# Weight block sums and residual additions moved from VectorE to accumulating DMAs, in a hybrid decoder layer on one Trainium2 core

## The chip, the core and the metric

The kernel runs on one core of one Trainium2 chip. A core has TensorE (PE: matmuls, with weight loads, PEld, running beside them), VectorE (DVE), ScalarE (ACT), GpSimd (POOL) and SyncE (SP), each with its own in-order queue of instructions; waits between them are semaphores. DMAs are issued from SP (all loads of weights) and from POOL, and run on 16 DMA engines.

The metric is the device time in microseconds. The kernel before takes 1687.98 us (median of three runs, 1686.88 to 1688.58).

## The reference

One decoder layer on 256 tokens of width 2048, all in float32:

```
x = layer_norm(ALPHA*x + 0.5 * swiglu_ffn(x, ffn1 weights))       # D_FF = 5632
u = x @ w_in + b_in ;  attention on 16 heads | conv module on 1024 channels
x = layer_norm(ALPHA*x + concat(attention, conv) @ w_out + b_out)
x = layer_norm(ALPHA*x + 0.5 * swiglu_ffn(x, ffn2 weights))
swiglu_ffn(x, g, u, d) = (silu(x @ g) * (x @ u)) @ d
```

Most of the arithmetic is in the two FFNs: per FFN three products with 2048 x 5632 weights.

## The kernel before

**Three matmuls per product.** Every float32 operand is split into a rounded part `hi` and a rest `lo = x - hi`. A product is hi*hi + hi*lo + lo*hi, three matmuls in the function `mm3` (L624 to L626). The split of a weight tile of 128 x 1024 costs one ScalarE cast (`upper`, L153: hi) and one VectorE subtraction (`lower`, L157: lo). Both halves go into rings of eight tiles; TensorE reads them from there.

**Seven products in place of eight.** In most of both FFNs the matrices are taken in 2 x 2 blocks. A step of kind "C" is the plain one: two weight tiles, eight block products. A step of kind "S" is a Strassen-like one: seven products, for which sums of the weights' blocks and of the activations' blocks are needed. One call of `by_sums` runs eight such steps with two of kind "S" (SCCSCCCC, once CCSCSCCC): 62 products in eight PSUM banks. A call computes either two groups of the up product (`pair`) or half of a down product's columns (`down_by_sums`). There are 28 calls, so 56 sets of weight tiles for "S" steps.

**A set.** `load_set` loads two weight tiles: one into `raw` (blocks a0 | a1), one into `rawx` (b0 | b1). Out of these VectorE makes the operands in four subtractions (`sub`, L171): t0 = b0 - a0, t1 = b1 - t0 (tiles `sum`), b0 = b1 - b0 in place in `rawx`, a1 = a1 - t1 in place in `raw`. The operands are taken in the order U0 = a0 | a1, U1 = t0 | t1, U2 = the changed rawx, U3 = the changed a1; each is split into hi and lo like any weight tile. Four buffers of kind `raw` are shared by all loads; a buffer is loaded anew when its last split is done (`ended`, `load`).

**What sets the order.** The class `Steps` writes out the order by hand. `jobs` is the list of splits still to be done, `pending` holds a `lo` until the next tile's `hi` has been queued, and `pace` takes jobs while a running estimate of VectorE's backlog is below a limit. `soon` holds short pieces of work (additions, the splits of activations) that `pace` slips in between; `at(n, work)` puts work n steps ahead. `can` lets a tile be split up to seven tiles ahead of the one in use.

**Evictions.** When a call's second "S" step has ended, `shared` combines the four banks that only "S" steps fill: in `pair` with VectorE additions at L1002 into tiles `part`, in `down_by_sums` with L881 into `part`, followed by four VectorE additions of these parts to the residual `xt` (`plus`, L885). The other four banks are added at the end of the call (L1002, L881). The next call's products reuse the banks.

**Activations.** At the end of a `pair` ScalarE applies silu to the parts (L1018), VectorE multiplies gate and up side (L949) and transposes 32 x 32 blocks (`turn`, L963), and POOL takes the result through DRAM: four DMAs `far<-hr` (L968) and one `hf<-far` (L970). Six steps later VectorE splits `hf` into `hh`, `hl` (L926, L977).

Of the kernel before, what the change touches and what calls it, by code (L numbers as in the profile page):

```python
# [74 lines left out]
class Steps:  # L75
# [6 lines left out]
    def __init__(self, nc, pool, sources, head, pooled, xT, x_raw, xcat):  # L82
# [3 lines left out]
        self.jobs, self.ready, self.pending, self.sets = [], {}, [], 0  # L86
        self.later, self.background, self.backlog = [], None, 0.0
# [24 lines left out]

    def load(self):
        while self.open < RAW_BUFS and self.loaded < len(self.sources):
            n = self.loaded
            if isinstance(self.sources[n], tuple):
                if self.sets == 2:
                    return
                self.load_set(n)
                continue  # L120
# [13 lines left out]
            self.jobs.append(("free", None, None))  # L134

    def load_set(self, n):
# [6 lines left out]
        for i, work in enumerate((self.zeroth, self.first, self.second, self.third)):  # L143
            self.jobs.append((n + i, raws, work))

# [24 lines left out]
    def sub(self, out, a, b):  # L170
        self.nc.vector.tensor_tensor(out=out, in0=a, in1=b, op=ALU.subtract)  # L171
        self.vector(0.6)

    def zeroth(self, n, raws):
        zero = self.upper(n, raws[0])
        self.flush()
        raws.append(zero)

    def first(self, n, raws):
        a, b = ([r[:, :512], r[:, 512:]] for r in raws[:2])  # L180
        t = [self.act.tile([P, 512], F32, tag="bc", name=f"sum{n}", bufs=BC) for _ in range(2)]
        raws.append(t)
        self.sub(t[0], b[0], a[0])
        self.sub(t[1], b[1], t[0])
        self.pending = [raws[2], self.upper(n, t)]

    def second(self, n, raws):
        b = [raws[1][:, :512], raws[1][:, 512:]]
        self.sub(b[0], b[1], b[0])
        self.pending.append(self.upper(n, raws[1]))  # L190
        self.flush(1)

    def third(self, n, raws):
        a1 = raws[0][:, 512:]
        self.sub(a1, a1, raws[3][1])
        three = self.upper(n, a1)
        self.flush(1)
# [7 lines left out]
        self.pending.append(ended)  # L205
# [124 lines left out]
def hybrid_layer(  # L330
# [534 lines left out]
    def down_by_sums(hh, hl, kinds, factor):  # L865
# [11 lines left out]
        for c in range(0, NC_, 2):  # L877
            ys = {(i, j): xt[:, 1 - i, (c + j) * 512 : (c + j + 1) * 512] for i in range(2) for j in range(2)}

            def add(out, ps, other):  # L880
                nc.vector.scalar_tensor_tensor(out=out, in0=ps, scalar=factor, in1=other, op0=ALU.mult, op1=ALU.add)  # L881
                st.vector(0.62, 0.3)

            def plus(y, t):
                nc.vector.tensor_tensor(out=y, in0=y, in1=t, op=ALU.add)  # L885
                st.vector(0.6)

            def shared(bank, ys=ys):
# [4 lines left out]
                add(tmp[3], bank[5], tmp[1])  # L893
                add(ys[1, 1], bank[5], ys[1, 1])
# [603 lines left out]
```

## Time and profile before

| | |
|---|---|
| median of three runs | 1687.98 us |
| the profiled execution's own time | 1688.99 us |
| its span, first to last instruction | 1687.2 us |
| granted TensorE clock, mean | 0.998 |
| DVE busy | 1386.7 us (82%), 2035 instructions |
| ACT busy | 912.9 us (54%) |
| POOL busy | 268.1 us (16%), nearly all between 680 and 980 us |
| DMA, mean rate | 213 GB/s |

A matmul's record is longer than the distance to the next matmul's start, because matmuls are pipelined and their ends are modelled; a busy share of TensorE therefore hides short stalls, and counting matmuls in a stretch shows them better. An entry such as "idle before 9.3 <-ACT hi" says how long the engine stood before the instructions of a group, and who ended most of it.

### The profile page before, as it was taken

Reading aid. Unit: us, or ns where it says so; the run is one execution under the profiler, and the core shown is the slowest. Engines: PE = TensorE matmul, PEld = TensorE weight load, DVE = VectorE, ACT = ScalarE, POOL = GpSimd, SP = SyncE. Lnnn points to the kernel's source line nnn. Section 1 sums busy time; section 2 is a strip of 40 time slices with the busy share of each in tenths; the row PEclk is TensorE's granted clock in tenths of the full one; section 3 lists DMA queues with packets and bytes.
Section 4 is the critical chain, followed back from the end, with each engine's and each line's share of the span. In section 5 each row is a group of like instructions: output and inputs, shape, how many; then the busy total and the mean of one; then the engine's idle time right before and its main releaser. Section 6 shows DMA issues by size and latency. Waiting matters only on the chain.

```text
span 1687.2 us, 21755 instructions
## 1 busy us (share of the span) xinstructions
PE 1669.7 (99%) x7689; PEld 1383.6 (82%) x7689; DVE 1386.7 (82%) x2035; ACT 912.9 (54%) x1252; POOL 268.1 (16%) x226
## 2 busy tenths in 40 slices
PE   9999999999999999999999999999999999999997
PEld 7887788888888888888888888877888888888886
DVE  7888898789888886758887778998888888988866
ACT  6556555555555554576665465555545555545541
POOL 0100000000000000178996200000000000000000
PEclk9999999999999999999999999999999999999999
DMA  8767666567666667556654555776656665666682
GB/s 295 241 211 271 219 209 218 191 223 244 214 215 211 212 213 246 171 182 194 200 181 157 198 193 196 246 236 210 219 200 215 221 237 202 222 200 224 209 279 99
DMA packets 103694, 359.47 MB, mean 213 GB/s; under 512 B 12960, under 2 KB 13088, under 8 KB 103328
## 3 DMA queue, kind: packets, MB, share of 16 engines
q1 hardware_dynamic: 96048, 334.74, 58.6%
q0 software_dynamic: 7392, 23.08, 4.5%
q8 instruction: 60, 0.98, 0.2%
q14 instruction: 50, 0.41, 0.1%
q10 hardware_dynamic: 144, 0.26, 0.0%
HBM read 344.40 MB, written 13.63 MB: 212 GB/s over the span
## 4 chain that ended last, share of the span: by engine, by line
PE 67%; DVE 19%; DMA 6%; issue 5%; ACT 3%; DVEq 0%; POOL 0%; ACTq 0%; SPq 0%; POOLq 0%
PE sum L624 13%; PE sum L625 13%; PE sum L626 13%; DVE lo L157 9%; PE acc L624 4%; PE acc L626 4%; PE acc L625 4%; DMA raw<-in_wu 3%; ACT hi L153 2%; DVE part L1002 2%; DVE sum L171 2%; PE in_c L1149 2%; PE in_a L1149 2%; PE in_q L1149 1%; DMA raw<-in_wd 1%
## 5 line engine op out<-in xcount | busy, mean ns | idle before, releaser
L157 DVE TENSOR_TENSOR lo<-raw,hi 128x1024 fp32r<-128x1024 f32 x452 | 506.6, 1153 | 121.5 <-ACT hi L153 121.0
L153 ACT CAST hi<-raw 128x1024 fp32r<-128x1024 f32 x452 | 432.9, 996 | 298.9 <-DMA raw<-in_wu 108.1
L624 PE MATMUL sum<-hi,xcat 128*128 128x512 f32 x1080 | 420.4, 389 | 1.6 <-DVE part L1002 1.6
L625 PE MATMUL sum<-lo,xcat 128*128 128x512 f32 x1080 | 420.3, 389 | 0.6 <-DVE lo L157 0.6
L626 PE MATMUL sum<-hi,xcat 128*128 128x512 f32 x1080 | 420.2, 389 | 0.0
L624 PEld LDWEIGHTS sum<-hi,xcat 128*128 128x128 f32 x1080 | 202.7, 188 | 44.7 <-DVE part L1002 2.5
L625 PEld LDWEIGHTS sum<-lo,xcat 128*128 128x128 f32 x1080 | 202.7, 188 | 42.9 <-DVE lo L157 1.0
L626 PEld LDWEIGHTS sum<-hi,xcat 128*128 128x128 f32 x1080 | 202.7, 188 | 42.2
L968 POOL DMA_DIRECT2D far<-hr x88 | 48.8, 556 | 1167.3 <-DVE hr L963 1120.9
L236 ACT CAST hi<-raw 128x1024 fp32r<-128x1024 f32 (+1 forms) x164 | 166.6, 1030 | 119.9 <-PE acc L626 71.8
L624 PE MATMUL sum<-hi,hh 128*128 128x512 f32 x496 | 194.0, 391 | 1.9 <-DVE part L1002 1.3
L239 POOL TENSOR_TENSOR lo<-raw,hi 128x1024 fp32r<-128x1024 f32 x73 | 175.6, 2423 | 117.5 <-ACT hi L236 110.6
L626 PE MATMUL sum<-hi,hl 128*128 128x512 f32 x496 | 193.1, 389 | 0.0
L625 PE MATMUL sum<-lo,hh 128*128 128x512 f32 x496 | 193.0, 389 | 0.0
L153 ACT CAST hi<-sum 128x512 fp32r<-128x512 f32 x112 | 69.5, 622 | 139.1 <-DVE sum L171 128.9
L239 DVE TENSOR_TENSOR lo<-raw,hi 128x1024 fp32r<-128x1024 f32 (+1 forms) x91 | 106.9, 1203 | 37.9 <-ACT hi L236 37.1
L1002 DVE TENSOR_TENSOR part<-sum,part 128x512 f32<-128x512 f32 x160 | 105.1, 685 | 12.7 <-PE sum L626 8.1
L624 PEld LDWEIGHTS sum<-hi,hh 128*128 128x128 f32 x496 | 93.1, 188 | 25.1 <-DVE part L1002 3.5
L626 PEld LDWEIGHTS sum<-hi,hl 128*128 128x128 f32 x496 | 93.1, 188 | 19.4
L625 PEld LDWEIGHTS sum<-lo,hh 128*128 128x128 f32 x496 | 93.1, 188 | 18.8
L1212 DVE SCALAR_TENSOR_TENSOR conv<-hc,cw_sb,conv 128x256 f32<-128x256 f32 x231 | 96.6, 482 | 1.1
L153 ACT CAST hi<-rawx 128x1024 fp32r<-128x1024 f32 x56 | 59.0, 1053 | 48.9 <-DVE rawx L171 39.3
(198 smaller groups left out, 2319.2 us busy)
## 6 DMA issues: line engine op xcount, KB each, us to landing
raw<-in_wu SPq DMA_DIRECT2D x308, 512.0 KB, 4.8
raw<-in_wd SPq DMA_DIRECT2D x160, 512.0 KB, 4.7
raw<-in_win SPq DMA_DIRECT2D x52, 512.0 KB, 4.1
rawx<-in_wu SPq DMA_DIRECT2D x40, 512.0 KB, 6.3
raw<-in_wout SPq DMA_DIRECT2D x32, 512.0 KB, 3.7
far<-hr POOLq DMA_DIRECT2D x88, 128.0 KB, 2.7
hf<-far POOLq DMA_DIRECT2D x22, 512.0 KB, 3.6
rawx<-in_wd SPq DMA_DIRECT2D x16, 512.0 KB, 6.4
```

The costliest lines, as they stand in the source:

```text
L153: self.nc.scalar.copy(hi, x_)
L157: self.nc.vector.tensor_tensor(out=lo, in0=x_, in1=hi.bitcast(F32), op=ALU.subtract)
L171: self.nc.vector.tensor_tensor(out=out, in0=a, in1=b, op=ALU.subtract)
L236: nc.scalar.copy(hi, raw)
L239: eng.tensor_tensor(out=lo, in0=raw, in1=hi.bitcast(F32), op=ALU.subtract)
L624: nc.tensor.matmul(ps, s_hi, m_hi, start=start, stop=False)
L625: nc.tensor.matmul(ps, s_hi, m_lo, start=False, stop=False)
L626: nc.tensor.matmul(ps, s_lo, m_hi, start=False, stop=stop)
L968: nc.gpsimd.dma_start(far[:, :, t].rearrange("f r n -> r f n"), hr[32 * t : 32 * t + 32])
L1002: nc.vector.tensor_tensor(out=out, in0=ps, in1=other, op=ALU.add)
L1149: nc.tensor.matmul(ps, w[0][:, n], x1[:, k], start=k == 0, stop=False)
L1212: nc.vector.scalar_tensor_tensor(out=out, in0=x_, scalar=w, in1=acc, op0=ALU.mult, op1=ALU.add)
```

## The change

The block sums get other signs, so that all of them are additions on the weights' side: t0 = a0 + b0 and t1 = t0 + b1 stay on VectorE (now `plus`, L183), b0 += b1 (in `rawx`) and a1 += t1 (in `raw`) become DMAs from SBUF to SBUF that add to their destination, issued on POOL's queue (L192 and L200 of the changed kernel). The activations' sums and the combination of the banks have their signs changed to fit, with as many instructions as before. In `down_by_sums` the four additions to the residual become four such DMAs (L912); the addition of bank 5 to the residual becomes one more part, so the number of L881 additions is the same.

The order changes with it. The two sums of a set are placed two weight tiles earlier. U3's split is held back until the next load has been put on the list, so it stands one weight tile later. Every `lo` now stays pending until the next tile's `hi` is queued. The DMAs through DRAM are queued one and three steps after the transpose in place of at once, and the split of `hf` after seven steps in place of six. Counted over the program, VectorE has 1893 instructions in place of 2037, POOL 375 in place of 231, of which 56 are b0 += b1, 56 a1 += t1 and 32 additions to the residual. TensorE's instructions are the same, in the same order.

```
@@ last_third, load
+    def last_third(self):
+        if self.held is not None:
+            self.jobs.append(self.held)
+            self.held = None
...
             if isinstance(self.sources[n], tuple):
                 if self.sets == 2:
                     return
+                self.last_third()
                 self.load_set(n)
                 continue
...
             self.get(raw, n, 0, 1024)
             self.jobs.append(("free", None, None))
+            self.last_third()
@@ load_set
-        for i, work in enumerate((self.zeroth, self.first, self.second, self.third)):
+        early = len(self.jobs) > 3 and self.jobs[-1][0] == "free"
+        at = len(self.jobs) - 2 if early else len(self.jobs)
+        self.jobs.insert(at, (n - early, raws, self.sums))
+        for i, work in enumerate((self.zeroth, self.first, self.second)):
             self.jobs.append((n + i, raws, work))
+        self.held = (n + 3, raws, self.third)
@@ the set's work
-    def sub(self, out, a, b):
-        self.nc.vector.tensor_tensor(out=out, in0=a, in1=b, op=ALU.subtract)
+    def plus(self, out, a, b):
+        self.nc.vector.tensor_tensor(out=out, in0=a, in1=b, op=ALU.add)
         self.vector(0.6)
+
+    def sums(self, n, raws):
+        a, b = ([r[:, :512], r[:, 512:]] for r in raws[:2])
+        t = [self.act.tile([P, 512], F32, tag="bc", name=f"sum{n}", bufs=BC) for _ in range(2)]
+        raws.append(t)
+        self.plus(t[0], a[0], b[0])
+        self.plus(t[1], t[0], b[1])
+        self.nc.gpsimd.dma_start(b[0], b[1], accum_op=ALU.add)
 
     def zeroth(self, n, raws):
         zero = self.upper(n, raws[0])
         self.flush()
-        raws.append(zero)
+
+        def ended():
+            zero()
+            self.nc.gpsimd.dma_start(raws[0][:, 512:], raws[2][1], accum_op=ALU.add)
+
+        self.pending = [ended]
 
     def first(self, n, raws):
-        a, b = ([r[:, :512], r[:, 512:]] for r in raws[:2])
-        t = [self.act.tile([P, 512], F32, tag="bc", name=f"sum{n}", bufs=BC) for _ in range(2)]
-        raws.append(t)
-        self.sub(t[0], b[0], a[0])
-        self.sub(t[1], b[1], t[0])
-        self.pending = [raws[2], self.upper(n, t)]
+        one = self.upper(n, raws[2])
+        self.flush()
+        self.pending = [one]
 
     def second(self, n, raws):
-        b = [raws[1][:, :512], raws[1][:, 512:]]
-        self.sub(b[0], b[1], b[0])
-        self.pending.append(self.upper(n, raws[1]))
-        self.flush(1)
+        two = self.upper(n, raws[1])
+        self.flush()
+        self.pending = [two]
 
     def third(self, n, raws):
-        a1 = raws[0][:, 512:]
-        self.sub(a1, a1, raws[3][1])
-        three = self.upper(n, a1)
-        self.flush(1)
+        three = self.upper(n, raws[0][:, 512:])
+        self.flush()
@@ down_by_sums
                 tmp = [act.tile([P, 512], F32, tag="z", name="part", bufs=ZB) for k in range(4)]
                 nc.scalar.mul(tmp[0], bank[1], factor)
                 add(tmp[1], bank[6], tmp[0])
-                add(tmp[3], bank[5], tmp[1])
-                add(ys[1, 1], bank[5], ys[1, 1])
+                add(tmp[3], bank[5], tmp[1], ALU.subtract)
                 add(tmp[2], bank[7], tmp[1])
-                for n, (at, k) in enumerate((((0, 0), 0), ((0, 1), 3), ((1, 0), 2), ((1, 1), 2))):
-                    st.soon.append(lambda y=ys[at], t=tmp[k]: plus(y, t))
+                add(tmp[1], bank[5], tmp[2], ALU.subtract)
+                for at, k in ((0, 0), 0), ((0, 1), 3), ((1, 0), 2), ((1, 1), 1):
+                    nc.gpsimd.dma_start(ys[at], tmp[k], accum_op=ALU.add)
@@ turn
-                    for t in range(4):
-                        nc.gpsimd.dma_start(far[:, :, t].rearrange("f r n -> r f n"), hr[32 * t : 32 * t + 32])
+                    def leave():
+                        for t in range(4):
+                            nc.gpsimd.dma_start(far[:, :, t].rearrange("f r n -> r f n"), hr[32 * t : 32 * t + 32])
+
                     hf = pool.tile([P, 8 * P], F32, tag="ht", name="hf")
-                    nc.gpsimd.dma_start(hf, far.rearrange("f r t n -> (f r) (t n)"))
+                    st.at(1, leave, True)
+                    st.at(3, lambda: nc.gpsimd.dma_start(hf, far.rearrange("f r t n -> (f r) (t n)")), True)
...
-                    st.at(6, lambda: st.soon.extend([lambda t=t: split(hf, t) for t in range(2)]))
+                    st.at(7, lambda: st.soon.extend([lambda t=t: split(hf, t) for t in range(2)]))
```

The first place is VectorE's queue in the first FFN, where the second `pair` ends: the first set of the third `pair` is split ahead, and the last row is the evictions at the second one's end, for which the third one's products wait. In the names, `lo<-raw` is a tile's split, `sum` is t0 and t1, and the brackets name the semaphores waited for: DMAHW a load's landing, DMASW the landing of a DMA of POOL's queue, Activation, PE and DVE these engines. Before:

```order
L171 TENSOR_TENSOR sum_1161<-rawx_1097,raw_1096 128x512 [waits DMAHW2_49,DMAHW1_49]
L171 TENSOR_TENSOR sum_1162<-rawx_1097,sum_1161 128x512 [waits DVE_49]
L157 TENSOR_TENSOR lo_1150<-raw_1096,hi_1149 128x1024 [waits Activation_49]
L171 TENSOR_TENSOR rawx_1097<-rawx_1097 128x512
L157 TENSOR_TENSOR lo_1166<-sum_1161,hi_1165 128x512 [waits Activation_49]
L157 TENSOR_TENSOR lo_1166<-sum_1162,hi_1165 128x512 [waits Activation_49]
L171 TENSOR_TENSOR raw_1096<-raw_1096,sum_1162 128x512 [waits DVE_49]
L157 TENSOR_TENSOR lo_1181<-rawx_1097,hi_1180 128x1024 [waits Activation_49]
L157 TENSOR_TENSOR lo_1197<-raw_1096,hi_1196 128x512 [waits Activation_49]
L157 TENSOR_TENSOR lo_1216<-raw_1132,hi_1215 128x1024 [waits DMAHW4_49,Activation_49]
L157 TENSOR_TENSOR lo_1236<-raw_1141,hi_1235 128x1024 [waits DMAHW5_49,Activation_49]
L1002 TENSOR_TENSOR part<-sum,part 128x512 [waits PE_49] x3
```

The same place in the changed kernel:

```order
L183 TENSOR_TENSOR sum_1140<-raw_1082,rawx_1083 128x512 [waits DMAHW2_49,DMAHW1_49]
L183 TENSOR_TENSOR sum_1141<-sum_1140,rawx_1083 128x512 [waits DVE_49]
L169 TENSOR_TENSOR lo_1138<-raw_1040,hi_1137 128x1024 [waits DMAHW7_49,Activation_49]
L169 TENSOR_TENSOR lo_1152<-raw_1058,hi_1151 128x1024 [waits DMAHW0_49,Activation_49]
L169 TENSOR_TENSOR lo_1164<-raw_1082,hi_1163 128x1024 [waits Activation_49]
L169 TENSOR_TENSOR lo_1173<-sum_1140,hi_1172 128x512 [waits Activation_49]
L169 TENSOR_TENSOR lo_1173<-sum_1141,hi_1172 128x512 [waits Activation_49]
L169 TENSOR_TENSOR lo_1185<-rawx_1083,hi_1184 128x1024 [waits DMASW2_49,Activation_49]
L169 TENSOR_TENSOR lo_1210<-raw_1087,hi_1209 128x1024 [waits DMAHW3_49,Activation_49]
L169 TENSOR_TENSOR lo_1213<-raw_1082,hi_1212 128x512 [waits DMASW3_49,Activation_49]
L169 TENSOR_TENSOR lo_1236<-raw_1155,hi_1235 128x1024 [waits DMAHW5_49,Activation_49]
L1020 TENSOR_TENSOR part<-sum,part 128x512 [waits PE_49] x3
```

The two in-place sums are gone, the two others stand two tiles earlier, ahead of `lo_1138` and `lo_1152`, and U2 (`lo_1185`) and U3 (`lo_1213`) now wait for DMAs of POOL's queue, U3 with one more tile ahead of it.

The second place is POOL's queue at a call's end in the first FFN. Before, it holds nothing but the way through DRAM:

```order
L968 DMA far<-hr 32x4x256 [waits DVE_49]
L968 DMA far<-hr 32x4x256 x3
L970 DMA hf<-far 128x1024 [waits DMASW6_49,DMASW7_49,DMASW5_49,DMASW0_49]
```

In the changed kernel, from the second set of the second `pair`, which is split while the first one's result passes, to the first set of the third:

```order
L192 DMA rawx_856<-rawx_856 128x512 [waits DMAHW0_49,DMASW6_49,DVE_49]
L984 DMA far<-hr 32x4x256 [waits DVE_49]
L984 DMA far<-hr 32x4x256 x2
L984 DMA far<-hr 32x4x256 [waits DMASW7_49]
L200 DMA raw_855<-sum_919 128x512 [waits DMASW2_49,DMAHW7_49,DMASW0_49,DVE_49]
L988 DMA hf<-far 128x1024 [waits DMASW6_49,DMASW5_49,DMASW7_49,DMASW4_49,DMASW1_49]
L192 DMA rawx_1083<-rawx_1083 128x512 [waits DMAHW2_49,DVE_49]
L200 DMA raw_1082<-sum_1141 128x512 [waits DMAHW1_49,DMASW3_49,DMAHW5_49,DMASW0_49,DVE_49]
```

The addition a1 += t1 (`raw_855<-sum_919`) stands behind the four `far<-hr` issues, and `hf<-far` behind it.

More of the change, by code (lines that the diff above doesn't have):

```diff
@@ L111, in raw @@
         return self.pool.tile([P, 1024], F32, tag="raw", name=f"raw{n}", bufs=RAW_BUFS)
+    def last_third(self):
+        if self.held is not None:
+            self.jobs.append(self.held)
+            self.held = None
     def load(self):
@@ L203, in ended @@
             self.load()
-        self.pending.append(ended)
+        self.pending = [ended]
     def split(self):
@@ L878, in down_by_sums, with add @@
             ys = {(i, j): xt[:, 1 - i, (c + j) * 512 : (c + j + 1) * 512] for i in range(2) for j in range(2)}
-            def add(out, ps, other):
-                nc.vector.scalar_tensor_tensor(out=out, in0=ps, scalar=factor, in1=other, op0=ALU.mult, op1=ALU.add)
+            def add(out, ps, other, op=ALU.add):
+                nc.vector.scalar_tensor_tensor(out=out, in0=ps, scalar=factor, in1=other, op0=ALU.mult, op1=op)
                 st.vector(0.62, 0.3)
-            def plus(y, t):
-                nc.vector.tensor_tensor(out=y, in0=y, in1=t, op=ALU.add)
-                st.vector(0.6)
             def shared(bank, ys=ys):
@@ L922, in block_sums @@
                 for o, y, z, op in (
-                    (out[:, 0], x_[0], x_[2], ALU.add), (out[:, 2], x_[1], x_[0], ALU.subtract),
-                    (out[:, 1], out[:, 0], x_[1], ALU.subtract), (out[:, 3], x_[3], out[:, 1], ALU.subtract),
+                    (out[:, 0], x_[0], x_[2], ALU.subtract), (out[:, 2], x_[1], x_[0], ALU.subtract),
+                    (out[:, 1], out[:, 0], x_[1], ALU.subtract), (out[:, 3], x_[3], out[:, 1], ALU.add),
                 ):
@@ L993, in split, with add @@
                         parted(at + 3, sums)
-                    st.at(6, lambda: st.soon.extend([lambda t=t: split(hf, t) for t in range(2)]))
+                    st.at(7, lambda: st.soon.extend([lambda t=t: split(hf, t) for t in range(2)]))
                 def pair(g, ups):
                     tmp, places = [], {(0, 0): 0, (0, 1): 2, (1, 0): 1, (1, 1): 3}
-                    def add(out, ps, other):
-                        nc.vector.tensor_tensor(out=out, in0=ps, in1=other, op=ALU.add)
+                    def add(out, ps, other, op=ALU.add):
+                        nc.vector.tensor_tensor(out=out, in0=ps, in1=other, op=op)
                         st.vector(0.62, 0.3)
@@ L1009, in shared @@
                         add(tmp[1], bank[6], tmp[0])
-                        add(tmp[2], bank[5], tmp[1])
+                        add(tmp[2], bank[5], tmp[1], ALU.subtract)
                         add(tmp[1], bank[7], tmp[1])
-                        add(tmp[3], bank[5], tmp[1])
+                        add(tmp[3], bank[5], tmp[1], ALU.subtract)
                     def out(at, ps):
```

## The prediction

> **What bounds the kernel now.** First the page's busy times.
>
> ```profile
> PE 1669.7 (99%) x7689; PEld 1383.6 (82%) x7689; DVE 1386.7 (82%) x2035; ACT 912.9 (54%) x1252; POOL 268.1 (16%) x226
> ```
>
> TensorE's 99% is no measure of its pace, since a record (0.39 us) is longer than the distance between two starts. That distance stands in the timeline of a stretch without stalls:
>
> ```profile
> 299.68 0.39 PE L626 MATMUL sum<-hi,xcat 128*128 128x512 f32 x1
> ...
> 300.36 0.39 PE L626 MATMUL sum<-hi,xcat 128*128 128x512 f32 x1
> ```
>
> Three matmuls, one product, in 0.68 us: 0.227 us each. The change leaves TensorE's work alone, so it can win only TensorE's stalls. The table of stretches shows where they are (after PE and (x), the number of matmuls that started or ran there; then PEld, DVE, ACT, POOL, clock, DMA share, GB/s):
>
> ```profile
> 42.20:84.40 42.20, 42.20 (x188) 34.95 (x187) 35.40 (x47) 23.17 (x31) 4.86 (x8) 1.00 0.73 241
> 126.50:168.70 42.20, 41.35 (x181) 33.56 (x180) 36.53 (x47) 26.29 (x31) 2.78 (x5) 1.00 0.75 271
> 168.70:210.90 42.20, 41.60 (x183) 33.73 (x182) 35.48 (x47) 21.59 (x29) 2.77 (x5) 1.00 0.63 219
> 210.90:253.10 42.20, 42.07 (x186) 34.36 (x185) 38.06 (x47) 21.60 (x25) 0.00 (x0) 1.00 0.60 209
> 1054.50:1096.70 42.20, 41.62 (x184) 34.10 (x183) 38.63 (x54) 23.00 (x31) 2.77 (x5) 1.00 0.72 246
> 1096.70:1138.90 42.20, 41.03 (x178) 32.95 (x177) 38.77 (x51) 25.02 (x34) 2.77 (x5) 1.00 0.71 236
> 1138.90:1181.00 42.10, 41.14 (x180) 33.40 (x179) 37.72 (x50) 21.96 (x29) 2.77 (x5) 1.00 0.63 210
> 1181.00:1223.20 42.20, 42.05 (x185) 34.25 (x185) 37.64 (x47) 22.58 (x26) 0.00 (x0) 1.00 0.64 219
> 1645.00:1687.20 42.20, 30.70 (x146) 25.59 (x144) 28.15 (x53) 6.96 (x8) 3.10 (x4) 0.90 0.29 99
> ```
>
> A full stretch holds 187 or 188. The seven short ones lack 6, 4, 1, 3, 9, 7 and 2 against 187: 32 matmuls, 32 x 0.227 = **7.3 us**. That is about all this change can win: the last row's idle time is the final normalisation, which isn't touched, and the other stretches of the FFNs are full. In the short ones VectorE is busy 35.5 to 38.8 us of 42.2, as the rows show, and what TensorE waits for is VectorE's evictions:
>
> ```profile
> 136.05 0.39 PE L626 MATMUL sum<-hi,xs 128*128 128x512 f32 x1
> 137.16 0.50 PE L624 MATMUL sum<-hi,xcat 128*128 128x512 f32 x1 [0.72 <-DVE part L1002]
> ```
>
> VectorE before that moment is hardly ever idle; this is a whole set, from its first block sum to the evictions:
>
> ```profile
> 126.48 0.68 DVE L171 TENSOR_TENSOR sum<-rawx,raw 128x512 f32<-128x512 f32 x1
> ...
> 128.94 0.68 DVE L171 TENSOR_TENSOR rawx<-rawx 128x512 f32<-128x512 f32 x1
> 129.55 1.28 DVE L157 TENSOR_TENSOR lo<-sum,hi 128x512 fp32r<-128x512 f32 x2
> 130.75 0.68 DVE L171 TENSOR_TENSOR raw<-raw,sum 128x512 f32<-128x512 f32 x1
> 131.35 1.22 DVE L157 TENSOR_TENSOR lo<-rawx,hi 128x1024 fp32r<-128x1024 f32 x1
> 133.20 0.69 DVE L157 TENSOR_TENSOR lo<-raw,hi 128x512 fp32r<-128x512 f32 x1 [0.63 <-ACT hi L153]
> 134.15 2.36 DVE L157 TENSOR_TENSOR lo<-raw,hi 128x1024 fp32r<-128x1024 f32 x2 [0.26 <-ACT hi L153]
> 136.43 2.48 DVE L1002 TENSOR_TENSOR part<-sum,part 128x512 f32<-128x512 f32 x4
> 140.33 1.23 DVE L157 TENSOR_TENSOR lo<-raw,hi 128x1024 fp32r<-128x1024 f32 x1 [1.43 <-ACT hi L153]
> ```
>
> The evictions stand behind the splits in VectorE's queue and come 7 us after the first split. So VectorE, late by up to a few microseconds here, is the bound behind TensorE in seven stretches, and nowhere else.
>
> **What is removed.** Two subtractions a set. From start to start one costs 0.6 us (128.94 to 129.55, 130.75 to 131.35), so 1.2 us a set, and 0.6 x 4 = 2.4 us in each down call for the additions to the residual. The groups by shape give their number, and the waits that go with them:
>
> ```profile
> L171 DVE TENSOR_TENSOR rawx<-rawx 128x512 f32<-128x512 f32 x56 | 38.3, 684 | 0.0
> L885 DVE TENSOR_TENSOR xt<-xt,part 128x512 f32<-128x512 f32 x32 | 19.9, 682 | 0.0
> L157 DVE TENSOR_TENSOR lo<-raw,hi 128x512 fp32r<-128x512 f32 x56 | 38.3, 685 | 9.3 <-ACT hi L153 9.3
> L157 DVE TENSOR_TENSOR lo<-rawx,hi 128x1024 fp32r<-128x1024 f32 x56 | 68.3, 1219 | 13.8 <-ACT hi L153 13.7
> L171 DVE TENSOR_TENSOR sum<-rawx,raw 128x512 f32<-128x512 f32 x56 | 37.8, 675 | 11.7 <-DMA rawx<-in_wd 7.1 <-DMA rawx<-in_wu 4.5
> L153 ACT CAST hi<-raw 128x512 fp32r<-128x512 f32 x56 | 34.8, 622 | 63.4 <-DVE raw L171 63.4
> ```
>
> VectorE stands (9.3 + 13.8) / 56 = 0.4 us a set because a tile that it changed itself must first go through ScalarE. These waits go too: **1.6 us a set saved**, two sets a call.
>
> **What is added.** The time of an adding DMA is nowhere in the trace. Nearest are POOL's own DMAs, from issue to landing:
>
> ```profile
> far<-hr POOLq DMA_DIRECT2D x88, 128.0 KB, 2.7
> hf<-far POOLq DMA_DIRECT2D x22, 512.0 KB, 3.6
> ```
>
> The view of the tile `hf` adds its spread:
>
> ```profile
> DMA to landing us min/median/max: 3.4/3.6/5.0
> ```
>
> An adding DMA of 256 KB reads 512 KB, source and destination, so I take 3.6 us, with 2.7 and 5.0 as ends. The addition to U3's half may start once U0's lo is done; until U3's turn VectorE has the two lo of U1 (129.55 to 130.75, 1.2), U2's and the next tile's (1.13 each): 3.5 us of cover. The chain is 3.6 + 0.62 for the half tile's cast: 4.2. VectorE stands 0.8 us, and 0.4 more because the next tile's cast (1.0) only starts behind it on ScalarE while U3's lo takes 0.6: **1.2 us a set**, from 0.2 (landing 2.7) to 2.6 (5.0). Behind that wait in VectorE's queue are the next lo and then the evictions for which TensorE waits. b0 += b1 has more cover (t1, two tiles, U0, U1: over 5 us) and costs nothing up to there.
>
> In a sentence by itself: the Trainium skill, "DMA: Bandwidth & Descriptors", section "Anatomy of one DMA — SWDGE (gpsimd) path", fits such a DMA by 2.0 us + bytes/436 GB/s, which makes an estimate of 2.6 us for 256 KB and would cut the wait to 0.2 us and clear all 7.3 us of stalls; here the fit gives 3.2 and 2.3 where the trace has 3.6 and 2.7, and it does not speak of adding.
>
> **What is moved.** The sums stand two tiles earlier and need the set's loads 2 x 1.13 = 2.3 us sooner. The list of waits (in total, times, longest) shows how many have no such margin today:
>
> ```profile
> DVE sum L171 <- DMA rawx<-in_wd: 7.1, 6, 1.4
> DVE sum L171 <- DMA rawx<-in_wu: 4.5, 7, 1.2
> ```
>
> These 13 of 56 sets pay all of it, 13 x 2.3 / 56 = 0.5 us a set, the others between nothing and 2.3, which no row tells: I take **0.6 us a set** (0.5 to 2.3), near the low end, since 43 sets don't wait at all. In an up call the second set's sums (1.3 us) come to stand right behind the evictions, where VectorE waits 1.43 us for a cast anyway (row 140.33): **1.3 us saved**. On POOL the same set's a1 += t1 stands behind four issues:
>
> ```profile
> L968 POOL DMA_DIRECT2D far<-hr x88 | 48.8, 556 | 1167.3 <-DVE hr L963 1120.9
> ```
>
> Four are 2.2 us, one lo (1.13) of which runs meanwhile: **1.1 us** per up call. `far` and `hf` leave later, and the split of `hf` is a step later; its activations are used only in the down call's last steps, many products on, so I cost that at nothing. U3's raw buffer is free one tile later: nothing while three others are filled, a load's wait if not.
>
> **The sum.** Up call: saved 3.2 + 1.3, new waits 2.4 + 1.2 + 1.1: -0.2, no gain, if every new wait delays VectorE in full. Down call: 3.2 + 2.4 - 2.4 - 1.2 = 2.0 gained. But the short stretches still hold 3.4 to 6.7 us of idle VectorE, so a new wait partly takes the place of one that comes anyway. Charged at half, an up call gains 2.1 us and a down call 3.8. That is more than any short stretch lacks per call (9 matmuls, 2.0 us), so all 7.3 us go. Charged in full, only the stalls behind a down call go, which are the short ones:
>
> ```profile
> PEld sum L624 <- DVE xt L881: 2.1, 5, 0.6
> ```
>
> In the table these are the stretches from 210.90 and 1181.00: 3 matmuls, 0.7 us. I take the middle of 7.3 and 0.7, **4.0 us**: 1688.99 - 4.0 = 1685.0 for a profiled execution; this one lay 1.0 over the median of the runs, so **1684.0 us**.
>
> **Rivals.** *A wash.* Every new wait counts in full, and VectorE is as late at the evictions as now. For it: both engines are in order, and U3's wait stands right ahead of the evictions. Against it: VectorE has half as many instructions for the sums. Gain -2 to 3 us: 1687.0 us.
>
> *Slower: the adding DMA lands late.* At 5.0 us (`hf`'s slowest) U3's wait is 2.6 us. Charged in full an up call loses 3.0 us (4.5 saved, 2 x 2.6 + 2.3 waited) and a down call 0.8; the seven short stretches hold about four up and three down calls: 4 x 3.0 + 3 x 0.8 = 14 us, 1702. At three quarters an up call loses 1.1 us and a down call nothing: 4 us, 1692. I put it at 1697. It decides where the charged waits reach the 4.5 us saved: a landing of 3.5 us in full, of 5.7 us at half. For it: the loads keep the engines two thirds busy (the 0.60 to 0.75 above) and reading the destination may be slower than I assume. The queues' row prices the traffic:
>
> ```profile
> q0 software_dynamic: 7392, 23.08, 4.5%
> ```
>
> (packets, MB, share of the 16 engines.) 144 DMAs of 0.262 MB are 37.7 MB, 7.4% of the engines, 15% with the second read, which takes the busiest short stretch from 0.75 to 0.90, so the engines don't become the bound.
>
> **How the numbers follow.** Within 0.2%, 3.4 us, a measurement of this kernel can't tell a change from none: 1684.6 to 1691.4. The forecast case (half or more of the stalls gone, 1680.5 to 1684.6) gets 0.41, the wash 0.32, slower 0.27. So faster 0.41, same 0.32, slower 0.27. Range: low end all 7.3 us and a little run-to-run, 1679.5; high end into the slower case, 1699. The likeliest case's own range is 1680.5 to 1684.6.
>
> **What would show it.** Right: the seven stretches at 187 matmuls, 144 fewer VectorE instructions (some 95 us less busy: 112 x 0.68 + 32 x 0.68), additions landing in 3 to 4 us, waits of U3's cast on them under 1 us. Wrong: landings of 5 us or more; ScalarE's casts waiting for POOL's DMAs by over 100 us in all; sums waiting for `rawx` far beyond 11.7 us; new short stretches where now there are 188.

## The result and the profile after

The changed kernel takes 1784.89 us (median of four runs, 1782.20 to 1788.64), the kernel before beside it 1688.28 us (four runs, 1686.88 to 1690.10): a ratio of 1.0573, 95% interval 1.0551 to 1.0595. It is **slower by 96.6 us**. The prediction said 1684.0 us, and 1699 at the high end; it was wrong in sign.

The page of the changed kernel: busy times, the queue of GpSimd's DMAs, the first line of the chain that ended last, and GpSimd's issues with their size and the median from issue to landing.

```profile
PE 1703.9 (96%) x7689; PEld 1393.6 (78%) x7689; DVE 1303.6 (73%) x1891; ACT 903.4 (51%) x1252; POOL 395.7 (22%) x370
q0 software_dynamic: 28128, 60.83, 17.0%
PE 32%; DMA 29%; DVE 16%; issue 13%; ACT 5%; POOL 3%; SPq 1%; ACTq 0%; DVEq 0%; POOLq 0%
rawx<-rawx POOLq DMA_DIRECT2D x56, 256.0 KB, 3.6
raw<-sum POOLq DMA_DIRECT2D x56, 256.0 KB, 4.5
xt<-part POOLq DMA_DIRECT2D x32, 256.0 KB, 7.4
```

The edit does what it says: VectorE has 144 instructions fewer and is busy 83 us less (1386.7 before). But the chain now runs through DMAs for 29% of the span; before, it was TensorE for 67% and DMAs for 6%:

```profile
PE 67%; DVE 19%; DMA 6%; issue 5%; ACT 3%; DVEq 0%; POOL 0%; ACTq 0%; SPq 0%; POOLq 0%
```

What the freed VectorE gave is not seen, and new waits are (engine, line and what it waited for; total, times, longest):

```profile
DVE lo L169 <- ACT hi L165: 266.5, 163, 7.7
ACT hi L165 <- DMA rawx<-rawx: 187.9, 53, 10.6
ACT hi L165 <- DMA raw<-sum: 183.2, 44, 7.5
DVE sum L183 <- DMA rawx<-in_wu: 55.3, 30, 5.0
DVE sum L183 <- DMA rawx<-in_wd: 26.5, 16, 3.0
PEld sum L643 <- DVE part L1020: 38.0, 25, 4.3
```

Three things are in it: ScalarE's casts wait 187.9 us for b0 += b1 and 183.2 us for a1 += t1, and the two sums left on VectorE wait 81.8 us for the set's loads, where it was 11.7 before. In the last line TensorE's weight loads wait for evictions, which come later for it. The table of stretches (same columns as in the prediction; a full one of 44.6 us holds 196 to 200 matmuls):

```profile
89.20:133.80 44.60, 39.69 (x159) 31.59 (x160) 34.14 (x43) 18.16 (x25) 5.50 (x9) 0.92 0.76 224
223.00:267.60 44.60, 39.30 (x163) 31.48 (x163) 28.19 (x33) 18.03 (x22) 5.76 (x7) 0.92 0.79 224
579.80:624.40 44.60, 44.60 (x199) 36.93 (x198) 34.28 (x41) 21.61 (x28) 5.77 (x8) 1.00 0.78 232
1248.80:1293.40 44.60, 38.95 (x162) 31.20 (x161) 28.89 (x34) 20.21 (x23) 5.63 (x8) 0.92 0.80 228
```

Of the seven stretches inside the FFNs with the fewest matmuls six lie behind a down call's residual additions; the first row here, the lowest of them, does not. In all seven even the granted clock is below 1.00, which it was nowhere inside the FFNs before. The timeline of a place behind the residual, GpSimd first, then VectorE, ScalarE and TensorE:

```profile
220.60 0.86 POOL L912 DMA_DIRECT2D xt<-part  x1 [9.77 <-ACT part L906]
222.70 1.74 POOL L912 DMA_DIRECT2D xt<-part  x2 [1.23 <-DVE part L900]
230.00 0.88 POOL L912 DMA_DIRECT2D xt<-part  x1 [5.56 <-issue]
230.95 0.87 POOL L192 DMA_DIRECT2D rawx<-rawx  x1
...
227.08 0.69 DVE L183 TENSOR_TENSOR sum<-sum,rawx 128x512 f32<-128x512 f32 x1
239.49 1.23 DVE L169 TENSOR_TENSOR lo<-rawx,hi 128x1024 fp32r<-128x1024 f32 x1 [7.10 <-ACT hi L165]
...
238.41 1.04 ACT L165 CAST hi<-rawx 128x1024 fp32r<-128x1024 f32 x1 [9.98 <-DMA rawx<-rawx]
...
244.24 0.80 PE L643 MATMUL sum<-hi,hh 128*128 128x512 f32 x1 [2.74 <-DVE xt L900]
```

The set's second sum ends at 227.8. b0 += b1 could go then, but GpSimd is still at the residual: it stands 5.56 us between the third and the fourth of those DMAs, with no semaphore to wait for ("issue"). So b0 += b1 is issued at 230.95 and needs 7.3 us to land behind the four transfers; U2's cast is at 238.41, VectorE has stood 7.10 us, and the evictions (`xt`, L900) come so late that TensorE stands too.

### The profile page after: what moved, and what is told of

It is laid out like the page before. It is cut to its first block, busy times and chain, and to the rows that moved or that the text cites. A ratio compares the mean times of both kernels' runs of the same rounds, so it can differ in the third digit from the quotient of the medians.

```text
span 1783.4 us, 22067 instructions
## 1 busy us (share of the span) xinstructions
PE 1703.9 (96%) x7689; PEld 1393.6 (78%) x7689; DVE 1303.6 (73%) x1891; ACT 903.4 (51%) x1252; POOL 395.7 (22%) x370
## 3 DMA queue, kind: packets, MB, share of 16 engines
q0 software_dynamic: 28128, 60.83, 17.0%
## 4 chain that ended last, share of the span: by engine, by line
PE 32%; DMA 29%; DVE 16%; issue 13%; ACT 5%; POOL 3%; SPq 1%; ACTq 0%; DVEq 0%; POOLq 0%
DMA raw<-sum 9%; DVE lo L169 8%; DMA rawx<-in_wu 7%; DMA raw<-in_wu 5%; ACT hi L165 4%; PE acc L643 4%; PE acc L645 4%; PE acc L644 4%; DMA rawx<-rawx 3%; PE sum L644 3%; PE sum L643 3%; PE sum L645 3%; DMA rawx<-in_wd 3%; DVE part L1020 2%; PE in_c L1167 2%
## 5 line engine op out<-in xcount | busy, mean ns | idle before, releaser
L169 DVE TENSOR_TENSOR lo<-raw,hi 128x1024 fp32r<-128x1024 f32 (+1 forms) x452 | 508.1, 1153 | 198.7 <-ACT hi L165 198.5
L165 ACT CAST hi<-raw 128x1024 fp32r<-128x1024 f32 (+1 forms) x452 | 431.8, 994 | 358.9 <-DMA raw<-sum 183.2
L643 PE MATMUL sum<-hi,xcat 128*128 128x512 f32 x1080 | 425.9, 394 | 32.7 <-DVE part L1020 19.7
L644 PE MATMUL sum<-lo,xcat 128*128 128x512 f32 x1080 | 424.9, 393 | 4.2 <-DVE lo L169 4.1
L645 PE MATMUL sum<-hi,xcat 128*128 128x512 f32 x1080 | 423.7, 392 | 0.0
L645 PEld LDWEIGHTS sum<-hi,xcat 128*128 128x128 f32 x1080 | 204.6, 189 | 42.5
L255 ACT CAST hi<-raw 128x1024 fp32r<-128x1024 f32 (+1 forms) x164 | 166.3, 1030 | 116.0 <-PE acc L645 61.4
L643 PE MATMUL sum<-hi,hh 128*128 128x512 f32 x496 | 198.1, 399 | 24.4 <-DVE xt L900 11.0
L192 POOL DMA_DIRECT2D rawx<-rawx x56 | 48.9, 874 | 756.6 <-DVE sum L183 736.4
L644 PE MATMUL sum<-lo,hh 128*128 128x512 f32 x496 | 196.9, 397 | 3.1 <-DVE lo L169 3.0
L165 ACT CAST hi<-rawx 128x1024 fp32r<-128x1024 f32 x56 | 58.9, 1052 | 195.1 <-DMA rawx<-rawx 187.9
L258 DVE TENSOR_TENSOR lo<-raw,hi 128x1024 fp32r<-128x1024 f32 (+1 forms) x91 | 107.1, 1202 | 37.1 <-ACT hi L255 36.3
L169 DVE TENSOR_TENSOR lo<-rawx,hi 128x1024 fp32r<-128x1024 f32 x56 | 68.4, 1221 | 68.0 <-ACT hi L165 68.0
L183 DVE TENSOR_TENSOR sum<-raw,rawx 128x512 f32<-128x512 f32 x56 | 38.7, 691 | 81.8 <-DMA rawx<-in_wu 55.3
```

The costliest lines, as they stand in the source:

```text
L165: self.nc.scalar.copy(hi, x_)
L169: self.nc.vector.tensor_tensor(out=lo, in0=x_, in1=hi.bitcast(F32), op=ALU.subtract)
L183: self.nc.vector.tensor_tensor(out=out, in0=a, in1=b, op=ALU.add)
L192: self.nc.gpsimd.dma_start(b[0], b[1], accum_op=ALU.add)
L255: nc.scalar.copy(hi, raw)
L258: eng.tensor_tensor(out=lo, in0=raw, in1=hi.bitcast(F32), op=ALU.subtract)
```

## The experiments

Times are medians; "before" is the kernel before on the same chip, 1687.3 to 1688.8 us in every group.

### In the changed order: which of the three parts costs?

**e1: the order alone, all additions back on VectorE.**

```
-        self.nc.gpsimd.dma_start(b[0], b[1], accum_op=ALU.add)
+        self.plus(b[0], b[0], b[1])
...
-            self.nc.gpsimd.dma_start(raws[0][:, 512:], raws[2][1], accum_op=ALU.add)
+            self.plus(raws[0][:, 512:], raws[0][:, 512:], raws[2][1])
...
-                    nc.gpsimd.dma_start(ys[at], tmp[k], accum_op=ALU.add)
+                    st.soon.append(lambda y=ys[at], t=tmp[k]: st.plus(y, y, t))
```

> The changed kernel's order, but all block sums and the additions to the residual on VectorE (no adding DMA at all). If the new order itself (sums two tiles earlier, U3 one tile later, the way through DRAM later) costs the time, over 1730 us. If the adding DMAs' landings and POOL's queue cost it, within 5 us of the kernel before: 1683 to 1693 us.

1736.96 us (1727.01 to 1746.85), ratio 1.0292 (1.0246 to 1.0338). Half of the loss is there without one adding DMA. The waits of the sums for their loads are as in the changed kernel:

```profile
DVE sum L183 <- DMA rawx<-in_wu: 60.0, 23, 4.5
DVE sum L183 <- DMA rawx<-in_wd: 24.1, 9, 3.0
```

And stretches fall short that held 187 and 188 matmuls in the kernel before:

```profile
379.80:422.00 42.20, 40.95 (x178) 32.76 (x177) 36.16 (x49) 20.59 (x28) 2.77 (x5) 1.00 0.58 193
464.20:506.40 42.20, 40.32 (x178) 33.07 (x177) 35.90 (x44) 21.37 (x26) 0.00 (x0) 1.00 0.59 210
```

**e2: only the weights' sums by DMA** (third piece of e1's diff).

> The weights' sums stay adding DMAs, the additions to the residual go back to VectorE. Theory 'queue': the four residual adds stand ahead of b0 += b1 on POOL in every down call, and the calls behind them (5th, 11th, 19th, 25th and the one after each) carry 45 of the 96 us lost: 1740 us. Theory 'waits': each set's own wait for its two landings carries it, 56 sets alike: at most 10 us better than the changed kernel, 1775 us.

1744.47 us, ratio 1.0342 (1.0325 to 1.0359): 7.5 us over e1, which is within e1's spread. b0 += b1 is covered in this order and a1 += t1 is not, as VectorE's waits for the casts of U2 and U3 show:

```profile
L169 DVE TENSOR_TENSOR lo<-rawx,hi 128x1024 fp32r<-128x1024 f32 x56 | 68.3, 1219 | 12.5 <-ACT hi L165 12.3
L169 DVE TENSOR_TENSOR lo<-raw,hi 128x512 fp32r<-128x512 f32 x56 | 38.8, 693 | 117.3 <-ACT hi L165 117.3
```

Against these waits VectorE is busy 64 us less than in e1 and stands 27 us less at the sums, so that little comes out. ScalarE's casts wait 326 us for the two DMAs here (371 in the changed kernel): such a total is no measure of what is lost.

**e3: only the residual by DMA** (first two pieces).

> Only the residual additions are adding DMAs, all weights' sums on VectorE in the changed order. Nothing waits for these DMAs before the call's end, so by both theories ('queue' and 'waits') the time is that of the kernel with the order alone, or up to 4 us better since VectorE has 32 instructions fewer. If the adding DMAs hurt by slowing the loads instead, over 1700 us.

1734.85 us, ratio 1.0278 (1.0259 to 1.0296): within e1's spread. So the parts do not add up. Over e1's 1736.96 the weights' DMAs cost 7.5 us, the residual's -2.1, and both together 47.9: **42.5 us arise only where both share GpSimd's queue** (to some 8 us, since e1's own interval is 41.5 to 57.0 over the kernel before). The traces put them where the residual stands ahead: of the 68.0 us that VectorE stands for U2's cast in the changed kernel, against 12.5 in e2, 56 lie at the eight sets behind the residual's DMAs.

**e4: more room for GpSimd's descriptors**, paid for with one buffer elsewhere (what that buffer costs alone was not run).

```
-dynamic_dma_scratch_size=1024
+dynamic_dma_scratch_size=2048
...
-HB = 5
+HB = 4
```

> The changed kernel with twice the room for descriptors of POOL's DMAs (2048 in place of 1024 bytes; to find the room the mixer has four in place of five convolution buffers). In the trace the fourth residual add is issued when the first has landed, 4 to 5.6 us after it could. If that is for want of room, the fourth is issued at once, b0 += b1 some 3.5 us sooner in the down calls, and the time is about 1765 us. If the queue's order alone holds it, no change: 1780 to 1789 us.

1761.47 us, ratio 1.0436 (1.0414 to 1.0458): 23.4 us less than the changed kernel. The same place in its timeline, GpSimd:

```profile
222.19 2.65 POOL L912 DMA_DIRECT2D xt<-part  x3 [1.15 <-DVE part L900]
227.21 0.86 POOL L192 DMA_DIRECT2D rawx<-rawx  x1 [2.37 <-DVE sum L183]
```

The gap of 5.56 us is gone: all four are issued in a row, and b0 += b1 follows its sums at once. So with 1024 bytes only three of these DMAs fit: in the changed kernel the fourth goes 0.3 us after the first has landed (here 220.60 + 9.1), and it does so in all eight places, though in the other seven the profile names a split of VectorE's as what ended the wait. VectorE's waits for U2's cast fall from 68.0 to 45.8 us with it. What is left of the 42.5 us, some 19, goes with the four transfers that still lie ahead of b0 += b1; that it lands late there is seen (7.6 us or more in seven of e4's eight places), but no run took this part away by itself.

**e6: U3 not held back** (as e1, with this).

```
-        self.held = (n + 3, raws, self.third)
+        self.jobs.append((n + 3, raws, self.third))
```

> As the run with the order alone (1737 us), but U3's split follows U2's at once, as before the change; the sums stay two tiles early. Theory 'early sums': 1725 to 1740 us. Theory 'U3 held': 1690 to 1700 us.

1742.70 us, ratio 1.0327 (1.0312 to 1.0342): no better than e1. Holding U3 is not what makes the order dear.

### Where the sums stand

**e5: as e1, but the sums behind both tiles ahead of the set**, right ahead of U0's lo, as in the kernel before. All else of the new order stays: U3 held, `far` and `hf` delayed.

```
-        early = len(self.jobs) > 3 and self.jobs[-1][0] == "free"
+        early = False
...
     def sums(self, n, raws):
+        self.flush()
```

> As the run with the order alone (everything on VectorE, 1737 us), but the sums of a set stand where they stood before the change, behind the two tiles that precede the set. Theory 'early sums': VectorE, in order, stands at the sums until both of the set's loads have landed (84 us in that run against 12 us before), with two landed tiles behind them: 1690 to 1700 us. Theory 'U3 held': the raw buffer comes free a tile later and so the next loads: no better than 1725 us.

1687.51 us (ten runs), ratio 0.9996 (0.9987 to 1.0005). The whole 49 us of e1 are gone: they come from the place of the sums, and the rest of the order costs nothing that ten runs can tell.

**e16: a middle place** (e5 without the `flush`): in 24 of 56 sets one lo stands behind the sums, in the others none; in e1 it is two in nearly all.

> The changed order with all additions on VectorE (as e1), but the two sums one tile later than there: only the lo of the tile ahead still stands behind them, so the set's loads are needed some 1.1 us sooner than in e5 and 1.1 us later than in e1. Theory (what e1's 49 us come from is the loads of a set, which land just in time): between the two, 1695 to 1720, with 25 to 60 us of sums waiting for rawx. Rival (anything else in the changed order): no different from e5, 1687, or from e1, 1737.

1688.40 us (ten runs), ratio 0.9998 (0.9987 to 1.0009); the sums' waits for loads, then those of e5 are 2.9 and 2.8:

```profile
DVE sum L183 <- DMA rawx<-in_wu: 7.1, 5, 2.0
DVE sum L183 <- DMA rawx<-in_wd: 4.2, 6, 1.0
```

I had expected something between e5 and e1; there was no loss at all. So there is an edge: 24 of 56 sets 1.1 us sooner is free, nearly all of them 2.3 us sooner costs 49 us, with the waits for loads going from 11.3 to 84.1 us.

### Behind late sums: what does a DMA cost there?

**e7: the changed kernel with the sums late** (e5's diff alone).

> The changed kernel with all its adding DMAs, the sums at their old place behind two tiles. By 'early sums' the 48 us that the order cost go, less what b0 += b1 then lacks in cover (it had some 5.6 us of VectorE's work, now 3.1 us): 1745 to 1760 us. By 'U3 held' it isn't better than 1780 us.

1791.59 us, ratio 1.0618 (1.0601 to 1.0635): putting the sums back does not save the change, where I had expected 1745 to 1760. (The number is what "U3 held" forecast, but e5 and e6 rule that out.) Now the casts of U2 alone wait 253.7 us for their DMA. The latency is paid on one side or the other: ahead of the sums for loads, or behind them for additions.

**e12: the same without the residual's DMAs**; **e13: b0 += b1 alone**; **e14: a1 += t1 alone**. Each is e5 with one or two pieces of e1's diff taken back.

> The order of e5 with the weights' two adding DMAs a set, residual additions on VectorE: e7 without the residual's 32 DMAs. Theory (sharing POOL's queue with the residual's additions is some 43 us of e7's 104): 1735 to 1750. Rival (with sums at the old place the weights' DMAs alone cost nearly all of it, because their landing lies wholly behind the sums): 1765 to 1790.

> The order of e5, with b0 += b1 alone as an adding DMA; a1 += t1 and the residual on VectorE. Theory (in e12 the waits of the casts are all for this DMA, 232.6 us, and none for the other, so b0 += b1 has almost no cover): 1770 to 1785. Rival (both DMAs of a set cost alike): 1725 to 1745. By my prediction's step (b0 += b1 costs nothing): below 1690.

> The order of e5, with a1 += t1 alone as an adding DMA. Theory (U3's cast is three tiles behind and covers most of the landing): 1688 to 1705. Rival (both DMAs of a set cost alike): 1725 to 1745.

e12: 1784.00 us, ratio 1.0570 (1.0555 to 1.0584), where the rival had it: without the residual's DMAs nearly all of e7's loss stays. e13: 1781.78 us, ratio 1.0555 (1.0539 to 1.0571). e14: 1699.35 us, ratio 1.0061 (1.0048 to 1.0074). Nearly all lies in b0 += b1: 93 us alone, 97 with a1 += t1, which alone costs 11. The timeline of e13, GpSimd, ScalarE, VectorE:

```profile
279.48 0.85 POOL L193 DMA_DIRECT2D rawx<-rawx  x1 [24.55 <-DVE sum L183]
...
284.67 1.05 ACT L165 CAST hi<-rawx 128x1024 fp32r<-128x1024 f32 x1 [4.45 <-DMA rawx<-rawx]
...
281.35 1.29 DVE L169 TENSOR_TENSOR lo<-sum,hi 128x512 fp32r<-128x512 f32 x2
285.75 1.23 DVE L169 TENSOR_TENSOR lo<-rawx,hi 128x1024 fp32r<-128x1024 f32 x1 [3.12 <-ACT hi L165]
```

VectorE is through with U0 and U1 at 282.6, 3.1 us after the issue; the cast can start 5.2 us after it. The groups by shape, b0's lo in e5, in e13 and in the changed kernel:

```profile
L169 DVE TENSOR_TENSOR lo<-rawx,hi 128x1024 fp32r<-128x1024 f32 x56 | 68.2, 1218 | 1.5 <-ACT hi L165 1.5
```

```profile
L169 DVE TENSOR_TENSOR lo<-rawx,hi 128x1024 fp32r<-128x1024 f32 x56 | 68.6, 1226 | 167.8 <-ACT hi L165 167.8
```

```profile
L169 DVE TENSOR_TENSOR lo<-rawx,hi 128x1024 fp32r<-128x1024 f32 x56 | 68.4, 1221 | 68.0 <-ACT hi L165 68.0
```

167.8 us are 3.0 us a set, and 93 of them (1.7 a set) reach the end of the kernel. In e14 VectorE stands 64.5 us for U3's cast, 1.15 us a set, and 11 of them reach it.

**e8: the residual alone, in the kernel before.**

```
-                    st.soon.append(lambda y=ys[at], t=tmp[k]: plus(y, t))
+                    nc.gpsimd.dma_start(ys[at], tmp[k], accum_op=ALU.add)
```

> The kernel before, its order and all its weights' sums kept, with only the four additions to the residual per down call as adding DMAs (POOL has nothing else to do there). VectorE has 32 instructions less, 2.4 us per down call. If VectorE's lateness in the down calls is what it saves: 2 to 4 us faster than before, 1684 us. If the adding DMAs' traffic delays the loads: 0 to 5 us slower.

1692.57 us (eleven runs), ratio 1.0032 (1.0015 to 1.0050): a little slower, where the prediction had counted 2.4 us of VectorE a call as saved. GpSimd stands between these DMAs here too (33.6 us as "issue", 15 times), and the sums wait 19.6 us for their loads in place of 11.7.

### Is it the adding, the transfer, or GpSimd?

**e11: the changed kernel with copies in place of additions** (the additions are left out); **e17: the same for e12.**

```
-        self.nc.gpsimd.dma_start(b[0], b[1], accum_op=ALU.add)
+        self.nc.gpsimd.dma_start(b[0], b[1])
```

> The changed kernel with plain copying DMAs in the places of the 144 adding ones, same bytes, same queue, same waits; the additions themselves are left out (a block is overwritten by the other addend). Theory A (reading the destination for the addition is what makes these transfers slow): landings of 256 KB fall from 3.6 and 4.5 us to under 3.0, the queue's share from 17.0% to under 13%, and the time falls to 1750 or less. Theory B (latency, issue and ring room of POOL's queue, whatever is transferred): landings within 0.5 us of the adding ones and 1770 to 1785 us.

> e12 (sums late, the weights' two DMAs, residual on VectorE) with copying DMAs in the place of the adding ones; the two additions are left out (a block is overwritten by the other addend). Theory (what counts behind the late sums is the time from the second sum to the landing, 5.4 us there; a copy lands in 2.3 and issues in 0.55): the loss of 97 us falls by more than half, to 1700 to 1735, and VectorE's lo of rawx waits under 120 us in place of 214. Rival (issue and semaphores are the cost, not the transfer): over 1760.

e11: 1720.57 us (two runs), ratio 1.0193 (1.0175 to 1.0212), 64 us less than with additions. e17: 1757.60 us, ratio 1.0412 (1.0395 to 1.0429), 26 us less than e12: the smaller half of the loss, near the rival. The queue, the fourth DMA of the residual, an issue and the landing in e11:

```profile
q0 software_dynamic: 18912, 60.83, 10.3%
220.55 0.54 POOL L912 DMA_DIRECT2D xt<-part  x1 [0.19 <-issue]
L192 POOL DMA_DIRECT2D rawx<-rawx x56 | 30.6, 546 | 719.7 <-DVE sum L183 719.7
rawx<-rawx POOLq DMA_DIRECT2D x56, 256.0 KB, 2.3
```

An adding DMA of the same bytes has 144 packets where a copy has 80 ((28128 - 7392) / 144 and (18912 - 7392) / 144), takes 0.87 us of GpSimd to issue where the copy takes 0.55, and lands in 3.6 where the copy lands in 2.3. Nor does a fourth copy wait for the first to land, so e11 also leaves out the stall that e4 takes away, and its 64 us are not the price of the adding alone. And the copy's 2.3 us holds only for early sums: in e17 the same DMA lands in 4.0, where e12's adding one lands in 4.5. So e17 won less than I expected, and VectorE still stands 183.3 us for U2's cast, 214.3 in e12. Why the copy lands later there is not shown.

**e9 and e10: GpSimd computes the sums itself**, no DMA; the base is e5, in e9 b0 += b1, in e10 a1 += t1 too.

```
-        self.plus(b[0], b[0], b[1])
+        self.nc.gpsimd.tensor_tensor(out=b[0], in0=b[0], in1=b[1], op=ALU.add)
```

> The order of e5 (sums behind both tiles ahead), but b0 += b1 is an instruction that GpSimd itself computes, not a DMA; the other sums and the residual stay on VectorE. Theory (the adding DMA's time from issue to landing, and POOL's queue, are what costs behind the sums, and VectorE's time is worth little in this kernel): a GpSimd sum that ends within 3 us of VectorE's a0 += t0 and a1 += t1 moves nothing: 1685 to 1689 us. Rival (VectorE's time ahead of the sums is worth the 7 us of short stretches): 1680 to 1683. Second rival (GpSimd and VectorE hinder each other on these rows, so that sums and evictions stretch): over 1692.

> As e9_pool_adds_b0, with a1 += t1 computed by GpSimd as well, so that VectorE has half of the weights' sums as in the changed kernel, but no adding DMA is in it. Theory: within 3 us of e9, since the two GpSimd sums end before the casts that wait for them; 1684 to 1691. Rival (two GpSimd sums in a row end later than VectorE's would, and U3's cast is late): 1695 to 1720.

e9: 1701.97 us, ratio 1.0080 (1.0067 to 1.0094); e10: 1716.66 us, ratio 1.0169 (1.0155 to 1.0183). Of e9's expectations it was the second rival that came, and e10, which I had put within 3 us of e9, lost as much again: the groups show VectorE's own instructions getting longer. First e9, then e10:

```profile
L169 DVE TENSOR_TENSOR lo<-raw,hi 128x1024 fp32r<-128x1024 f32 x396 | 514.5, 1316 | 120.2 <-ACT hi L165 119.1
L183 DVE TENSOR_TENSOR raw<-raw,sum 128x512 f32<-128x512 f32 x56 | 62.3, 1113 | 1.9
```

```profile
L169 DVE TENSOR_TENSOR lo<-sum,hi 128x512 fp32r<-128x512 f32 x112 | 157.0, 1440 | 0.3 <-ACT hi L165 0.3
```

In the kernel before these take 1219, 685 and 683 ns on average. In e9 VectorE is spared 56 sums (38 us) and pays 396 x 0.097 = 38 us in the splits and 56 x 0.428 = 24 in its own a1 += t1. In e10 that sum leaves it too, and the splits of U1 take 112 x 0.757 = 85 us more. In all VectorE is busy 1390.8 us in e5, 1418.0 in e9 and 1441.3 in e10. The Trainium skill, "SBUF — State Buffer", section "SBUF: two separate sides", says that GpSimd and a VectorE instruction with two SBUF inputs take a shared pair of ports in turn, the one blocking the other for a whole instruction; these rows agree.

**e15: GpSimd computes the residual's additions, in the kernel before.**

```
-                    st.soon.append(lambda y=ys[at], t=tmp[k]: plus(y, t))
+                    nc.gpsimd.tensor_tensor(out=ys[at], in0=ys[at], in1=tmp[k], op=ALU.add)
```

> The kernel before, with a down call's four additions to the residual as GpSimd instructions of about 1.6 us in place of VectorE's or of DMAs; nothing else is changed. Theory (VectorE's time ahead of the sums behind a down call is worth a little, and e8's loss came from the DMAs' landing of 8.4 us): 1683 to 1687. Rival (the short stretches are ended by something else, so nothing is won): 1687 to 1690. Second rival (far and hf, queued behind them on GpSimd, come late): over 1692.

1699.81 us (six runs), ratio 1.0065 (1.0052 to 1.0078). It was meant to tell whether VectorE's time ahead of the sums is worth anything, and cannot: VectorE is hindered here too (the first sum of a set takes 818 ns on average, 675 before). Why it costs 11 us is not settled.

No version ran faster than the kernel before; the nearest are e5 and e16, which equal it.

## Why the prediction was wrong

**The step that failed first: "I take 0.6 us a set ..., near the low end, since 43 sets don't wait at all".** That a set does not wait says nothing about how much sooner it could go. The order alone costs 49 us (e1), 0.9 us a set at the end of the kernel, and all of it comes from the sums' place (e5). The waits for loads are 84 us, 1.5 a set; its own upper end, 2.3, contained them. It was also weighed against VectorE's savings in the seven short stretches only, as if the other stretches had slack; e1 made stretches short that were full.

**The step that failed second: "b0 += b1 has more cover (t1, two tiles, U0, U1: over 5 us) and costs nothing up to there".** With the queue free the cover is there (12.5 us of waits in 56 sets of e2), though t1 is no part of it, since the DMA goes when t1 is done: two tiles, U0 and U1 are 4.6 us, just what the landing (3.5 in e2) and U2's cast (1.05) take. But it is the early place of the sums that gives it, and that place costs 49 us. At the old place it is U0 and U1, 3.1 us, and the same DMA costs 93 us (e13). Cover and load margin are one and the same time, and I counted it twice.

**What was left out: the queue.** The prediction put a1 += t1 behind `far` on GpSimd, but never asked what the four residual additions stand ahead of. It is the next set's b0 += b1, eight times in the kernel. This is the 42.5 us that e1, e2 and e3 leave, 23.4 of them by the room for descriptors (e4). It also used one landing time for all three kinds of DMA: 3.6 was right for b0 += b1, a1 += t1 needs 4.5, and the residual's, issued in a bunch, 7.4.

**"Charged at half."** The halving of new waits had no row behind it, and both ends that the forecast was the middle of were gains (7.3 and 0.7 us). What came out was uneven, 93 of e13's 167.8 us of waits and 11 of e14's 64.5, and no run shows a gain from VectorE's saved time to set against it: in e14 it is busy 31 us less than in e5. The sums for the rivals also charged the new waits in the seven short stretches alone, as if the full ones could take them for nothing.

**Right:** 144 instructions fewer; VectorE's busy time down (83 us; 95 forecast); the landing of b0 += b1; the engines of the DMAs did not become the bound (17.0% on this queue, 12.5 more than before, forecast 15; 0.79 or so in the worst stretches); the delays of the way through DRAM cost nothing (they are in e5). U3's wait was sized 1.2 us a set, and VectorE stands 1.15 a set where a1 += t1 is the only adding DMA (e14, landing in 3.3 us) and 2.0 in the changed kernel (112.0 us over 56 sets, within the bounds of 0.2 to 2.6):

```profile
L169 DVE TENSOR_TENSOR lo<-raw,hi 128x512 fp32r<-128x512 f32 x56 | 38.7, 691 | 112.0 <-ACT hi L165 112.0
```

The rival "slower" had the sign, and a mechanism that is in the trace (U3's cast waiting for a DMA), but at 1697 it was a tenth of the loss: by e14 that mechanism is worth some 11 us. The signs named for "wrong" came: casts waiting over 100 us for GpSimd's DMAs (371), sums waiting far beyond 11.7 us (81.8), new short stretches. Whether the 7.3 us of short stretches could have been won at all by relieving VectorE stays open, since no run relieved it without a new wait or a hindrance.

The sum as the runs have it: 49.6 for the early sums (e1), 7.5 for the weights' DMAs behind them (e2), -2.1 for the residual's (e3), 42.5 for both in one queue: 97.5, against 1687.38 us of before beside these runs. By e1's interval the first term is known to about 8 us, and the last with it; the two small ones are not clear of it.

## What to carry to other kernels

Moving work to an asynchronous unit replaces a short cost with a latency, so find the consumer first and measure how much time lies between producer and consumer; moving the producer earlier to make that time only shifts the question to what the producer itself waits for, and "does not wait today" is not a margin. When an edit adds DMAs to a queue, list for each what follows it in that queue at every place of the program, and test the parts alone and together: here three parts cost 49.6, 7.5 and -2.1 us, and their meeting 42.5.

## What the hardware showed that was not expected

**Stalls halve TensorE's clock for a while.** The stretch of the timeline above in pieces of 1.7 us (TensorE's busy time and matmuls, granted clock, DMA share, GB/s):

```profile
237.10:238.80 1.70, 0.61 (x3) 1.00 0.54 96
238.80:240.50 1.70, 0.49 (x1) 1.00 0.03 5
240.50:242.20 1.70, 0.73 (x2) 0.77 0.00 0
242.20:243.90 1.70, 0.00 (x0) 0.50 0.57 176
243.90:245.60 1.70, 1.36 (x3) 0.50 1.02 371
245.60:247.30 1.70, 1.70 (x5) 0.50 0.99 349
247.30:249.00 1.70, 1.70 (x7) 0.72 0.84 335
```

From about 241.4 to 248.2 the clock is at 0.50, and matmuls follow each other in 0.43 us in place of 0.23, up to 4 us after the stall has ended (at 244.24). The trace has ten such pieces inside the FFNs, of 3.4 or 6.8 us, 51 us in all; the kernel before has none there. Mean clock 0.984 in place of 0.998 over 1783 us is at most some 25 us: up to a quarter of the loss is not stall but its echo. The Trainium skill, "TensorE: Matmul & The Clock Gate", section "Part 1: The HAM clock gate", states that an idle window of about 3.4 us halves the clock until a busy one has passed; the 6.8 us here are about two such windows, so the trace agrees, though the 3.4 us ahead of the drop were not empty: three matmuls started in them. The prediction priced a stall at its own length.

**A queue of DMAs can hold its engine with no semaphore in sight.** With a room for descriptors of 1024 bytes the fourth adding DMA went 0.3 us after the first had landed, eight times of eight, once shown as 5.56 us of "issue". With the room doubled it went at once, which was worth 23.4 us; and four copies (e11) went in a row in 1024 bytes.

**An adding DMA is dearer than its bytes**: 144 packets against 80, 0.87 us against 0.55 to issue, 12.5% of the engines for 37.7 MB against 5.8% as copies. The Trainium skill's fit that the prediction cites (an estimate of 2.6 us for 256 KB) lies near the 2.3 us of e11's copy of b0; the adding ones took 3.6 to 7.4.
